# The output projection of a hybrid decoder block as seven half-size block products, with the sums of its operands on GpSimd and the row normalization one step earlier

## The chip, the core and the metric

The kernel runs on one core of a Trainium2 chip. The core has five engines that run their own instruction streams and wait for each other by semaphores: PE (TensorE, matmuls and transposes), DVE (VectorE), ACT (ScalarE), POOL (GpSimd) and SP (SyncE, which here only issues DMAs). The metric is the time of one execution on the device in microseconds, as the median of several runs. Names such as L167 are lines of the kernel before.

## What is computed

One decoder block on x of 1024 x 1024 in float32: two kinds of attention, their outputs gated and summed to y, an output projection with a residual, and a SwiGLU feed-forward with a residual. This is the part that matters:

```python
y = jax.nn.sigmoid(g_a) * (o_a @ w_o_swa[l]) + jax.nn.sigmoid(g_b) * (o_b @ w_o_mla[l])
x = x + y @ w_out[l]

h = rmsnorm(x, ffn_norm_g[l])
x = x + (jax.nn.silu(h @ w_gate[l]) * (h @ w_up[l])) @ w_down[l]
```

## The kernel before

**Products in three.** A float32 product is made of three matmuls in the format fp32r: an operand is split into a high part, a cast by ACT, and a low part, the operand less its high part, on DVE (`split`, L159), and `mm3` (L163) multiplies high by high, high by low and low by high into one PSUM bank. Every operand of every product costs one cast on ACT and one subtraction on DVE, which reads the operand and its high part, both in SBUF unless the operand is fresh in PSUM.

**Mix stage (L1302 to L1355).** Twelve steps, named in `steps` (L1317), make y transposed, 128 features by 1024 tokens at a time: step `a4` to `a7` the gated product with `w_o_swa`, step `b0` to `b7` (`mix_b`) the product with `w_o_mla`, its gate, the sum and the split of y. For features 0 to 3 the first gate's product is one POOL operation (L1308). Every half of 512 tokens costs 12 matmuls.

**Output projection (L1505 to L1549).** Four segments, each half of the rows by half of the columns, in row blocks of 128: eight blocks of y by w_out, three matmuls each, into a bank; DVE adds the bank to x (`add`, L1528). w_out comes in pieces by the class `Stream`, three rounds of four pieces of 128 x 1024, each split when it is next. In segments 1 and 3 a row is then complete: ACT makes its sum of squares (L1534), POOL two small operations (`rstd_of`, L299 and L302), DVE the normalized row `xn` (L1539). One row block later `to_h` (L1365) transposes it on PE, eight transposes, and makes the operands of the feed-forward.

**Feed-forward.** The class `Seven` multiplies by a scheme in which a 2 x 2 block product takes seven block products instead of eight, with sums of blocks as operands. A pair of column blocks has the index j, its seven products the numbers q, and each comes for the gate weights (g) and the up weights (u); `fa(0,5)` means the bank `fa`, pair 0, product 5. The weight sums are made by `mix` and their splits by `prep`; the sums of the activations (`t1` to `t4`) are made by `to_h`, its second part `rest` (held back by L1547), and `late_split` (L1497), from the raw copies `hraw`. In before the sums and low parts of the activations are on DVE, the weight sums of pair 0 on POOL, of pair 1 on DVE (`ffn.mix(1, nc.vector)`).

**What sets the order.** On SP the program's order. On the other engines a scheduler places the work by its own costs, but from segment 3 on, through the first products of the feed-forward, the order is the one written out by hand (`manual_schedule`, L1505). Each engine runs its instructions in its order, so an instruction that waits holds up all behind it.

Of the kernel before, what the change touches and what calls it, by code (L numbers as in the profile page):

```python
# [89 lines left out]
def hybrid_block_kernel(  # L90
# [1248 lines left out]
    new_quads("y")  # L1339
    for k, (what, dc) in enumerate(steps):  # L1340
# [11 lines left out]
        if k >= 8:  # L1352
            st.load_to(st.index[("out", 0, k - 8)])
        if k >= 9:
            st.conv_to(st.index[("out", 0, min(k - 9, 3))])  # L1355
    st.conv_to(st.index[("out", 0, 3)])


    fg_bc = bcast_gain("ffng", ffn_g)
# [5 lines left out]
    def to_h(xn, b):  # L1365
# [140 lines left out]
    prev = None  # L1506
    held = []
    for seg, (sh, hf) in enumerate(((0, 0), (0, 1), (1, 1), (1, 0))):
        if seg == 3:
# [4 lines left out]
        hs = half(hf)
        for b in range(4 * sh, 4 * sh + 4):
            if seg in (0, 2):
                x2[b] = load_x(b)
# [10 lines left out]
            add(x2[b][:, hs], ps, x2[b][:, hs], nc.vector)  # L1528
            if seg in (0, 2):
                st.conv_to(st.index[("out", seg // 2 + 1, b % 4)])  # L1530
            if seg in (1, 3):
                xn = U("xn")
                ss = tiny("ss")
                nc.scalar.activation(xn, x2[b], AF.Square, accum_out=ss)  # L1534
                rs = rstd_of(ss, D)
            lower = to_h(*prev) if prev is not None else None
            prev = None
            if seg in (1, 3):
                nc.vector.scalar_tensor_tensor(xn, x2[b], rs, fg_bc, op0=ALU.mult, op1=ALU.mult)  # L1539
                prev = (xn, b)  # L1540
                nc.sync.dma_start(x2_d[b], x2.pop(b))
# [10 lines left out]
    held.pop(0)()
    ffn.run()
    ffn.prep_to(4)
    held.pop(0)()
# [133 lines left out]
def _layouts(a):  # L1689
# [80 lines left out]
```

## Time and profile before

| | us |
|---|---|
| median of 3 runs (lowest, highest) | 1362.41 (1362.39, 1362.61) |
| span of the profiled execution | 1359.5 |
| PE busy in the span | 1339.6 (99%) |
| DVE, ACT, POOL busy | 912.7, 642.8, 557.7 |
| first matmul of the output projection, from the span's start | 627.06 |

The span is one profiled execution, from its first instruction to its last; the runs' times are those of whole executions. A timeline row has the start and the duration in us, the engine, the line, the operation, the tile written and those read, and, in brackets, how long the engine had been idle and what ended that. A group of rows has busy us, mean ns of one instruction, and the idle time before them. Names of tiles have no buffer numbers.

### The profile page before, as it was taken

To read this page: it belongs to the slowest core of one execution; us is meant where nothing else is said; L and a number is where in the kernel's file an instruction comes from. 1 tells how busy PE (TensorE), PEld (TensorE's weight loads), DVE (VectorE), ACT (ScalarE), POOL (GpSimd) and SP (SyncE) were. 2 spreads that over 40 slices of the span, in tenths; PEclk is the share of its full clock that TensorE was granted. 3 is DMA by queue.
4 is the path that set the end of the run, shared out by engine and by line. 5 is a ranking of instruction groups with operands and counts; after the bars stand their busy time and mean duration, and the time that the engine had idled before them with its cause. 6 is when DMAs were issued, how large, how long until landed. Compare 5 with 4: busy or idle time off the path is not lost.

```text
span 1359.5 us, 18989 instructions
## 1 busy us (share of the span) xinstructions
PE 1339.6 (99%) x6600; PEld 1120.0 (82%) x6600; DVE 912.7 (67%) x1495; ACT 642.8 (47%) x1299; POOL 557.7 (41%) x610
## 2 busy tenths in 40 slices
PE   9999999999999999999999999999999999999997
PEld 6899878878788888888887888888888888888886
DVE  7868767676777887585448866666656654664862
ACT  7434766675577776652336322323232332644453
POOL 2116645553166554200031465766665551022521
PEclk9999999999999999999999999999999999999999
DMA  9455322335100110671243353644434425996504
GB/s 366 154 189 163 119 86 82 113 117 182 51 2 13 44 47 17 241 239 63 105 174 132 119 181 139 235 178 169 152 144 171 170 83 183 375 382 246 170 9 147
DMA packets 78096, 202.25 MB, mean 149 GB/s; under 512 B 8753, under 2 KB 15409, under 8 KB 78001
## 3 DMA queue, kind: packets, MB, share of 16 engines
q1 hardware_dynamic: 77856, 201.04, 41.5%
q8 instruction: 52, 0.85, 0.3%
q14 instruction: 44, 0.35, 0.1%
q10 hardware_dynamic: 144, 0.00, 0.0%
HBM read 141.24 MB, written 59.77 MB: 148 GB/s over the span
## 4 chain that ended last, share of the span: by engine, by line
PE 88%; DVE 4%; issue 3%; POOL 2%; ACT 2%; DMA 0%; SPq 0%; POOLq 0%; ACTq 0%; DVEq 0%
PE fa L169 7%; PE fa L167 7%; PE fa L168 7%; PE fb L169 6%; PE fb L167 6%; PE fb L168 6%; PE fd L167 5%; PE fd L169 5%; PE fd L168 5%; PE pTb L1165 2%; PE xo L169 2%; PE xo L167 2%; PE xo L168 2%; PE ob L1188 1%; PE oA L167 1%
## 5 line engine op out<-in xcount | busy, mean ns | idle before, releaser
L161 DVE TENSOR_TENSOR wl<-wr,wl 128x512 fp32r<-128x512 f32 x150 | 153.6, 1048 | 72.2 <-ACT wl L160 71.9
L161 DVE TENSOR_TENSOR lrv<-lr,lrv 128x1024 fp32r<-128x1024 f32 x77 | 105.2, 1397 | 49.9 <-ACT lrv L160 48.8
L160 ACT CAST lrv<-lr 128x1024 fp32r<-128x1024 f32 x77 | 80.3, 1054 | 96.0 <-PE fd L169 56.0
L167 PE MATMUL fd<-lrv 128*128 128x512 f32 x308 | 119.8, 389 | 0.0
L168 PE MATMUL fd<-lrv 128*128 128x512 f32 x308 | 119.8, 389 | 0.0
L169 PE MATMUL fd<-lrv 128*128 128x512 f32 x308 | 119.8, 389 | 0.0
L172 POOL TENSOR_TENSOR wr<-wr,sm 128x512 f32<-128x512 f32 (+1 forms) x38 | 46.4, 1229 | 149.1 <-DVE wl L161 116.4
L160 ACT CAST wl<-wr 128x512 fp32r<-128x512 f32 x150 | 87.0, 624 | 2.4 <-DVE wr L820 2.2
L299 POOL TENSOR_SCALAR ms<-ss 128x1 f32<-128x1 f32 x32 | 8.8, 274 | 189.1 <-ACT xn L1534 111.7
L161 DVE TENSOR_TENSOR wl<-sm,wl 128x512 fp32r<-128x512 f32 x60 | 47.5, 818 | 45.1 <-ACT wl L160 45.0
L169 PEld LDWEIGHTS fd<-lrv 128*128 128x128 f32 x308 | 57.8, 188 | 12.1
L168 PEld LDWEIGHTS fd<-lrv 128*128 128x128 f32 x308 | 57.8, 188 | 12.1
L167 PEld LDWEIGHTS fd<-lrv 128*128 128x128 f32 x308 | 57.8, 188 | 11.8
L1150 POOL TENSOR_TENSOR denb<-denb,neg_one 128x1 f32<-128x1 f32 x64 | 36.5, 571 | 74.4 <-ACT p L1149 64.7
L1149 ACT ACTIVATE p<-scb,nmb 128x384 f32<-128x384 f32 (+3 forms) x64 | 47.6, 745 | 35.9 <-DVE nmb L1148 34.1
L161 DVE TENSOR_TENSOR ptl<-pTb,pth 128x512 fp32r<-128x512 f32 (+2 forms) x96 | 50.1, 550 | 13.8 <-ACT pth L160 13.0
L1148 DVE CUSTOM_DVE_ANT_0 scb<-scb,mask 128x384 f32<-128x384 f32 (+3 forms) x64 | 48.6, 759 | 14.0 <-PE scb L1140 13.7
L1426 ACT ACTIVATE act<-sm 128x512 f32<-128x512 f32 x11 | 7.0, 636 | 104.8 <-DVE sm L175 104.8
L1151 POOL TENSOR_SCALAR p<-p,denb 128x384 f32<-128x384 f32 (+3 forms) x64 | 49.8, 778 | 6.3
L160 ACT CAST pth<-pTb 128x512 fp32r<-128x512 f32 (+2 forms) x96 | 43.0, 483 | 13.6 <-PE pTb L1165 13.1
L167 PE MATMUL fb<-t2h,wl 128*128 128x512 f32 x120 | 47.4, 395 | 0.0
L167 PE MATMUL fb<-t3h,wl 128*128 128x512 f32 x120 | 47.3, 394 | 0.0
(346 smaller groups left out, 4287.3 us busy)
## 6 DMA issues: line engine op xcount, KB each, us to landing
lr<-la_d SPq DMA_DIRECT2D x77, 256.0 KB, 5.4
wr<-in_w_gate_dram SPq DMA_DIRECT2D x22, 512.0 KB, 3.8
wr<-in_w_up_dram SPq DMA_DIRECT2D x22, 512.0 KB, 5.0
wd<-in_w_down_dram SPq DMA_DIRECT2D x22, 512.0 KB, 6.8
rb_d<-wd SPq DMA_DIRECT2D x22, 512.0 KB, 2.6
la_d<-sd SPq DMA_DIRECT2D x22, 512.0 KB, 5.4
lr<-rb_d SPq DMA_DIRECT2D x44, 256.0 KB, 5.4
lr<-in_w_down_dram SPq DMA_DIRECT2D x33, 256.0 KB, 5.6
```

What stands on the lines that cost most here:

```text
L160: nc.scalar.copy(hi, src)
L161: (eng or nc.vector).tensor_tensor(lo, src, hi.bitcast(F32), op=ALU.subtract)
L167: nc.tensor.matmul(ps, ah, bh, start=first and i == 0, stop=False, skip_group_check=go_on)
L168: nc.tensor.matmul(ps, ah, bl, start=False, stop=False, skip_group_check=go_on)
L169: nc.tensor.matmul(ps, al, bh, start=False, stop=last and i == n - 1, skip_group_check=go_on)
L172: eng.tensor_tensor(out, a, b, op=ALU.subtract)
L1148: nc.vector.tensor_tensor_reduce(s_, s_, m_, 1.0, -NEG, op0=ALU.add, op1=ALU.min, accum_out=nm)
L1149: nc.scalar.activation(p_, s_, AF.Exp, scale=-1.0, bias=nm, accum_out=den)
L1150: nc.gpsimd.tensor_tensor(den, den, neg_one[:, 0:1], op=ALU.pow)
L1151: nc.gpsimd.tensor_scalar(p[:, 0:w], p[:, 0:w], den, 0.0, op0=ALU.mult, op1=ALU.add)
L1165: nc.tensor.transpose(pp[:, i], p[:, blk(k0 + i)], ident)
L1188: nc.tensor.matmul(po[:, q_off:], vst, lo[:, kb % 4, q_off:], start=False, stop=kb == nk - 1)
```

## The change

**Output projection.** It becomes the scheme of the feed-forward: y (two blocks of rows by two of the inner dimension) times w_out (two by two) by seven products in the order 1, 2, 6, 7, 5, 4, 3. A product has four row blocks of twelve matmuls. Products share banks: 1 and 2, then 5 and 3, in banks A; 6, 7 and 4 in banks B. Product 1 is also kept in SBUF (`p1o`, four ACT copies) and added to x by POOL during products 6 and 7, and every other bank is added to x by DVE when a product ends in it.

**Sums and splits.** `y_sums` makes four sums for each of four pairs of feature blocks, 16 POOL operations of 128 x 512; `w_sum` eight POOL operations of 128 x 1024. Each product has its own splits of its operands (four of y and two of w_out, product by product), of which products 1 and 2 have theirs in the mix stage, and the others by a list (`prep`) that is worked off at 1.9 items for each row block. w_out is loaded in four pieces of 1 MB during the mix stage. The mix steps come in another order, with features dc and dc+4 as neighbours, and the layout of `w_o_mla` fits that.

**Rows.** `row_sum`, `row_norm` and `next_h` take the place of the chain behind segments 1 and 3: a row's squares are made when it is complete, its normalized values one row block later, its transposes after that. The last three rows' transposes stand between the first products of the feed-forward.

**Engines.** To POOL go one subtraction of `hraw`, the low parts of `t3` and `t4`, and the weight sums of pair 1; `to_h` makes its splits ahead of its copies of `hraw`.

The core of the diff:

```diff
-        for sh in range(2):
+        for sh in (1, 0):
             cs = half(sh)
             pb = PX("oB")
...
-            split(*hT(dc, cs), ga[:, cs])
-    steps = ("a4", "b0", "b1", "a5", "b2", "b3", "a6", "b4", "a7", "b5", "b6", "b7")
+        y[dc] = ga
+        y_split((1, 2)[dc // 4], dc % 4)
+        if dc >= 4:
+            y_sums(dc - 4)
...
+    def y_sums(k):
...
+        add(s1, a21, a22, nc.gpsimd)
+        sub(s3, a11, a21, nc.gpsimd)
+        sub(a21, s1, a11, nc.gpsimd)
+        sub(a11, a12, a21, nc.gpsimd)
...
+    def w_sum(n, j):
...
+        sub(*{1: (t1s[j], b12, b11), 3: (b12, b22, b12), 2: (b11, b22, t1s[j]), 4: (b21, b21, b11)}[n], nc.gpsimd)
...
+    steps = ("a4", "b0", "b4", "a5", "b1", "b5", "a6", "b2", "b6", "a7", "b3", "b7")
+    W_LOAD = {4: (0, 0), 5: (0, 1), 6: (1, 1), 8: (1, 0)}
+    W_WORK = {7: [(w_split, 1)], 9: [(w_sum, 1)], 10: [(w_sum, 3)], 11: [(w_split, 2), (w_sum, 2)]}
...
-        sub(r[:, 1], r[:, 1], t23[:, 0], nc.vector)
+        sub(r[:, 1], r[:, 1], t23[:, 0], nc.gpsimd)
...
-            split_h(name, c, r[:, i])
+            split_h(name, c, r[:, i], (nc.vector, nc.gpsimd)[i])
...
+    X_ORDER = (1, 2, 6, 7, 5, 4, 3)
...
+    def xo_done(q, t):
+        ps = bank["A" if q in (1, 2, 5, 3) else "B"][t]
+        if q == 1:
+            nc.scalar.copy(p1o[:, t], ps)
+        else:
+            residual(*{2: (4 + t, 0), 6: (4 + t, 1), 7: (t, 1), 5: (t, 1), 4: (t, 0), 3: (4 + t, 1)}[q], ps, nc.vector)
+        if q in (6, 7):
+            residual({6: 4, 7: 0}[q] + t, 1, p1o[:, t], nc.gpsimd)
+        if q == 7:
+            residual(t, 0, p1o[:, t], nc.gpsimd)
...
+    for q in X_ORDER:
...
+        for t in range(4):
...
+            if (q, t) == (5, 3):
                 ffn.mix(0)
...
+            mm3(bank["A" if q in (1, 2, 5, 3) else "B"][t],
+                [((ah[:, k, blk(t)], al[:, k, blk(t)]), (bh[:, k], bl[:, k])) for k in range(4)],
+                first=q in (1, 6, 5), go_on=q in (2, 7, 4, 3))
+            xo_done(q, t)
+            if q == 1 and t < 2:
+                w_sum(4, t)
+            n_x += q != 1
+            while prep and 30 - len(prep) < 1.9 * n_x:
+                f, q_, j = prep.pop(0)
+                f(q_, j)
+            r = {4: 0, 3: 4}.get(q)
+            if r is not None:
+                if q == 3:
+                    next_h()
+                row_sum(r + t)
+                if r + t >= 1:
+                    row_norm(r + t - 1)
+                if (q, t) == (4, 2):
+                    next_h()
...
     ffn.prep_to(14)
-    ffn.mix(1, nc.vector)
+    ffn.mix(1)
```

POOL in the mix stage and ahead of it, before: the last softmax normalizations of the attention (`p`), the four gate products (`sg<-ar,sg`), and behind them the small operations of the projection's rows.

```order
310 L1151 TENSOR_SCALAR p_6357<-p_6357,denb_6358 128x768
311 L1308 TENSOR_TENSOR sg_6510<-ar_6155,sg_6510 128x1024
312 L1308 TENSOR_TENSOR sg_6528<-ar_6195,sg_6528 128x1024
313 L1308 TENSOR_TENSOR sg_6601<-ar_6364,sg_6601 128x1024
314 L1308 TENSOR_TENSOR sg_6643<-ar_6448,sg_6643 128x1024
315 L299 TENSOR_SCALAR ms_7166<-ss_7164 128x1
316 L302 TENSOR_TENSOR rstd_7168<-ms_7166,neg_half 128x1
```

After, from the same gate product on. `ys` are the sums of y, `wt` and `wo` those of w_out; the pair of `sg` names in a row are features dc and dc+4.

```order
311 L1304 TENSOR_TENSOR sg_6510<-ar_6155,sg_6510 128x1024
312 L1304 TENSOR_TENSOR sg_6590<-ar_6195,sg_6590 128x1024
313 L175 TENSOR_TENSOR ys_6631<-sg_6510,sg_6508 128x512
314 L172 TENSOR_TENSOR ys_6632<-sg_6510 128x512
315 L172 TENSOR_TENSOR sg_6510<-ys_6631,sg_6510 128x512
316 L172 TENSOR_TENSOR sg_6510<-sg_6508,sg_6510 128x512
317 L1304 TENSOR_TENSOR sg_6713<-ar_6364,sg_6713 128x1024
318 L172 TENSOR_TENSOR ys_6632<-sg_6590 128x512
319 L175 TENSOR_TENSOR ys_6631<-sg_6590,sg_6552 128x512
320 L172 TENSOR_TENSOR sg_6590<-ys_6631,sg_6590 128x512
321 L172 TENSOR_TENSOR sg_6590<-sg_6552,sg_6590 128x512
322 L1304 TENSOR_TENSOR sg_6842<-ar_6448,sg_6842 128x1024
```

Between and behind the gate products stand the sums; sixteen of y, and six of w_out before the last of these.

DVE at the start of the feed-forward, before: `pu` and `sm<-fb` are evictions of the bank `fb` (products 6 and 7), `t1l` and `t4l` low parts of the activations' sums, `wl` low parts of weights, `sm<-wr` weight sums. `wl_7938` and `wl_7941` are the operands of `fa(0,5)`.

```order
1030 L175 TENSOR_TENSOR pu_7747<-fb_7920,pu_7747 128x512
1031 L161 TENSOR_TENSOR t1l_7870<-hraw_7379,t1h_7869 128x4x128
1032 L161 TENSOR_TENSOR t4l_7874<-hraw_7379,t4h_7873 128x4x128
1033 L161 TENSOR_TENSOR wl_7938<-sm_7458,wl_7938 128x512
1034 L161 TENSOR_TENSOR wl_7941<-sm_7462,wl_7941 128x512
1035 L175 TENSOR_TENSOR sm_7944<-wr_7707,wr_7710 128x512
1036 L175 TENSOR_TENSOR sm_7458<-fb_7902,pu_7726 128x512
1037 L172 TENSOR_TENSOR sm_7944<-sm_7944,wr_7707 128x512
1038 L172 TENSOR_TENSOR wr_7707<-wr_7707 128x4x128
```

After, the same products; the operands of `fa(0,5)` are `wl_7984` and `wl_7987`.

```order
1036 L175 TENSOR_TENSOR pu_7729<-fb_7932,pu_7729 128x512
1037 L161 TENSOR_TENSOR t1l_7903<-hraw_7594,t1h_7902 128x4x128
1038 L161 TENSOR_TENSOR wl_7951<-wr_7325,wl_7951 128x512
1039 L175 TENSOR_TENSOR sm_7387<-fb_7910,pu_7709 128x512
1040 L161 TENSOR_TENSOR t1l_7903<-hraw_7636,t1h_7902 128x4x128
1041 L161 TENSOR_TENSOR wl_7999<-wr_7347,wl_7999 128x512
1042 L161 TENSOR_TENSOR wl_8002<-wr_7348,wl_8002 128x512
1043 L175 TENSOR_TENSOR sm_7391<-fb_7932,pu_7729 128x512
1044 L161 TENSOR_TENSOR wl_7984<-sm_7387,wl_7984 128x512
1045 L161 TENSOR_TENSOR wl_7987<-sm_7391,wl_7987 128x512
```

The `t4l` and the `sm<-wr` sums have left DVE, the `wl` of `fa(0,5)` stand behind both evictions of product 7, and the `wl` of `fa(0,5)` and `fb(0,4)` have changed places.

PE at the same place, before: `fa(0,5)` for gate runs whole.

```order
3558 L169 MATMUL fb_7920<-t3h_7580,wl_7882 128x512
3559 L167 MATMUL fa_7985<-t1h_7869,wl_7938 128x512
3560 L168 MATMUL fa_7985<-t1l_7870,wl_7938 128x512
3561 L169 MATMUL fa_7985<-t1h_7869,wl_7938 128x512
3562 L167 MATMUL fa_7985<-t1h_7869,wl_7938 128x512
3563 L168 MATMUL fa_7985<-t1l_7870,wl_7938 128x512
```

After, right behind the last matmul of `fb(0,7)` for up: two matmuls each of `fa(0,5)` for gate and up, three of `fb(0,4)`, and then the first L169 of `fa(0,5)`, the one that multiplies by the low part of `wl_7984`.

```order
3511 L167 MATMUL fa_8005<-t1h_7902,wl_7984 128x512
3512 L168 MATMUL fa_8005<-t1l_7903,wl_7984 128x512
3513 L167 MATMUL fa_8024<-t1h_7902,wl_7987 128x512
3514 L168 MATMUL fa_8024<-t1l_7903,wl_7987 128x512
3515 L167 MATMUL fb_7910<-t4h_7906,wl_7999 128x512
3516 L168 MATMUL fb_7910<-t4l_7907,wl_7999 128x512
3517 L169 MATMUL fb_7910<-t4h_7906,wl_7999 128x512
3518 L169 MATMUL fa_8005<-t1h_7902,wl_7984 128x512
3519 L167 MATMUL fa_8005<-t1h_7902,wl_7984 128x512
```

Seven matmuls now stand between the end of `fb(0,7)` and the first that reads the low part of `wl_7984`, and this order is the scheduler's, behind the written one's end.

POOL at the start of the feed-forward, after: low parts of `t3` and `t4`, the weight subtractions of pair 0 (`wr<-wr,sm`), and the sums of pair 1.

```order
372 L172 TENSOR_TENSOR t3l_7680<-t_1454_7805,t3h_7679 128x4x128
373 L172 TENSOR_TENSOR hraw_7636<-hraw_7636,t_1462_7860 128x512
374 L172 TENSOR_TENSOR t3l_7680<-t_1462_7860,t3h_7679 128x4x128
375 L161 TENSOR_TENSOR t4l_7907<-hraw_7494,t4h_7906 128x4x128
376 L161 TENSOR_TENSOR t4l_7907<-hraw_7549,t4h_7906 128x4x128
377 L172 TENSOR_TENSOR wr_7347<-wr_7347,sm_7387 128x4x128
378 L161 TENSOR_TENSOR t4l_7907<-hraw_7594,t4h_7906 128x4x128
379 L172 TENSOR_TENSOR wr_7348<-wr_7348,sm_7391 128x4x128
380 L161 TENSOR_TENSOR t4l_7907<-hraw_7636,t4h_7906 128x4x128
381 L175 TENSOR_TENSOR sm_7990<-wr_7523,wr_7568 128x512
382 L172 TENSOR_TENSOR sm_7990<-sm_7990,wr_7523 128x512
```

In before there stand between the last row's small operations and the first `wd` operation only four rows there, all of weights:

```order
335 L299 TENSOR_SCALAR ms_7685<-ss_7683 128x1
336 L302 TENSOR_TENSOR rstd_7687<-ms_7685,neg_half 128x1
337 L172 TENSOR_TENSOR wr_7421<-wr_7421,sm_7458 128x4x128
338 L172 TENSOR_TENSOR wr_7422<-wr_7422,sm_7462 128x4x128
339 L172 TENSOR_TENSOR wr_7710<-wr_7710,sm_7944 128x4x128
340 L172 TENSOR_TENSOR wr_7710<-wr_7710,sm_7948 128x4x128
341 L172 TENSOR_TENSOR wd_8019<-wd_8019 128x512
```

The rows of `t3l` and `t4l` and the sums `sm` have moved to POOL, ahead of the `wd` operations.

## Rows read from the trace of the kernel before

**Rows 1.** The page: its first line, and PE and POOL of its parts 1 and 2.

```profile
span 1359.5 us, 18989 instructions
...
PE 1339.6 (99%) x6600; PEld 1120.0 (82%) x6600; DVE 912.7 (67%) x1495; ACT 642.8 (47%) x1299; POOL 557.7 (41%) x610
...
PE   9999999999999999999999999999999999999997
...
POOL 2116645553166554200031465766665551022521
```

**Rows 2.** Stretches: busy us (count) of PE, PEld, DVE, ACT, POOL; clock, DMA share, GB/s.

```profile
567.00:627.07 60.07, 60.07 (x267) 49.76 (x266) 46.25 (x59) 32.41 (x39) 9.59 (x4) 1.00 0.66 233
627.07:727.00 99.93, 99.09 (x466) 82.36 (x465) 50.66 (x63) 30.32 (x54) 16.56 (x23) 1.00 0.33 127
727.00:800.00 73.00, 72.58 (x321) 59.00 (x320) 60.20 (x82) 30.39 (x55) 31.18 (x21) 1.00 0.36 124
```

**Rows 3.** What PE waited for, 690 to 900 us: us, times, longest.

```profile
PE tp L1372 <- DVE xn L1539: 0.8, 1, 0.8
PE fa L167 <- ACT wl L160: 0.3, 1, 0.3
PE fa L169 <- DVE wl L161: 0.2, 1, 0.2
```

**Rows 4.** Timeline of PE: start, us, line, operation, tiles.

```profile
627.06 0.39 PE L167 MATMUL xo<-wv,yh 128*128 128x512 f32 x1
...
656.98 0.39 PE L167 MATMUL xo<-wv,yh 128*128 128x512 f32 x1
...
659.70 1.03 PE L1372 MATMUL tp<-ident,xn 128*128 128x128 f32 x8
660.50 0.48 PE L167 MATMUL xo<-wv,yh 128*128 128x512 f32 x1
```

**Rows 5.** Groups by line and shape, 567.00 to 627.07: busy, mean ns, idle before.

```profile
L1308 POOL TENSOR_TENSOR sg<-ar,sg 128x1024 f32<-128x1024 f32 x4 | 9.6, 2408 | 24.1 <-ACT sg L1221 24.1
...
L161 DVE TENSOR_TENSOR wl<-wr,wh 128x1024 fp32r<-128x1024 f32 x4 | 4.9, 1220 | 0.6 <-ACT wh L160 0.6
```

**Rows 6.** Timelines of DVE and POOL, 786 to 797.

```profile
786.68 0.69 DVE L175 TENSOR_TENSOR sm<-fa,sm 128x512 f32<-128x512 f32 x1 [2.03 <-PE fa L169]
786.92 1.30 POOL L172 TENSOR_TENSOR sm<-sm,wr 128x512 f32<-128x512 f32 x1
...
791.25 3.31 POOL L172 TENSOR_TENSOR wd<-wd,wd 128x512 f32<-128x512 f32 x2
791.65 5.16 DVE L161 TENSOR_TENSOR wl<-wr,wl 128x512 fp32r<-128x512 f32 x3
```

**Rows 7.** Timelines of DVE and POOL, 574 to 582.

```profile
574.98 2.41 POOL L1308 TENSOR_TENSOR sg<-ar,sg 128x1024 f32<-128x1024 f32 x1 [3.19 <-ACT sg L1221]
575.73 2.20 DVE L161 TENSOR_TENSOR yl<-sg,yh 128x512 fp32r<-128x512 f32 x1 [0.69 <-ACT yh L160]
...
580.38 0.69 DVE L161 TENSOR_TENSOR yl<-sg,yh 128x512 fp32r<-128x512 f32 x1
```

**Rows 8.** DMA issues from 560 to 800: KB each, median us to landing.

```profile
wr<-in_w_out_dram SPq DMA_DIRECT2D x12, 512.0 KB, 6.7
```

**Rows 9.** Timelines of PE and DVE at a row of the projection's end.

```profile
701.41 0.39 PE L167 MATMUL xo<-wv,yh 128*128 128x512 f32 x1
701.61 0.69 DVE L175 TENSOR_TENSOR x<-xo,x 128x512 f32<-128x512 f32 x1 [3.62 <-PE xo L169]
...
704.57 1.28 DVE L1539 SCALAR_TENSOR_TENSOR xn<-x,rstd,ffng 128x1024 f32<-128x1024 f32 x1 [2.27 <-POOL rstd L302]
```

**Rows 10.** Timelines of DVE, POOL and PE, 753 to 757.

```profile
753.13 1.29 DVE L161 TENSOR_TENSOR wl<-sm,wl 128x512 fp32r<-128x512 f32 x2
...
756.45 2.13 POOL L172 TENSOR_TENSOR wr<-wr,sm 128x512 f32<-128x512 f32 x1 [25.93 <-DVE sm L172]
756.56 0.39 PE L167 MATMUL fa<-t1h,wl 128*128 128x512 f32 x1
```

More of the change, by code (lines that the diff above doesn't have):

```diff
@@ L1302, in mix_b @@
     def mix_b(dc):
-        if dc % 2 == 0:
-            wo["b"] = st.get(("ob", dc // 2))
+        if dc < 4:
+            wo["b"] = st.get(("ob", dc))
         w = wo["b"]
@@ new lines, in y_sums, with w_load @@
+    def y_sums(k):
+        if k == 0:
+            y_new.extend([V("ys") for _ in range(2)])
+        s1, s3 = y_new[0][:, k], y_new[1][:, k]
+        a21, a11, a22, a12 = y[k][:, half(0)], y[k][:, half(1)], y[4 + k][:, half(0)], y[4 + k][:, half(1)]
+        add(s1, a21, a22, nc.gpsimd)
+        sub(s3, a11, a21, nc.gpsimd)
+        sub(a21, s1, a11, nc.gpsimd)
+        sub(a11, a12, a21, nc.gpsimd)
+    wr, wl, t1s = {}, {}, {}
+    def w_load(i, d):
+        wr[(i, d)] = V("wo")
+        nc.sync.dma_start(wr[(i, d)], w_out[i, d])
@@ new lines, in w_split @@
+    def w_split(q, j):
+        k = slice(2 * j, 2 * j + 2)
+        if j == 0:
+            wl[q] = (V("woh", F32R), V("wol", F32R))
+        key = {1: (0, 0), 2: (1, 0), 6: (0, 0), 7: (0, 1), 5: None, 4: (1, 0), 3: (1, 1)}[q]
+        hi, lo = wl[q]
+        split(hi[:, k], lo[:, k], t1s[j] if q == 5 else wr[key][:, k])
+    def w_sum(n, j):
+        k = slice(2 * j, 2 * j + 2)
+        if n == 1:
+            t1s[j] = U("wt", F32, (P, 2, 512))
+        b11, b12, b21, b22 = (wr.get((i, d)) for i in range(2) for d in range(2))
+        b11, b12, b21, b22 = (None if w is None else w[:, k] for w in (b11, b12, b21, b22))
+        sub(*{1: (t1s[j], b12, b11), 3: (b12, b22, b12), 2: (b11, b22, t1s[j]), 4: (b21, b21, b11)}[n], nc.gpsimd)
@@ L1328, in weights_of @@
         if k < len(steps):
-            return st.index[("o" + steps[k][0], int(steps[k][1]) // 2)]
+            what, dc = steps[k][0], int(steps[k][1])
+            return st.index[("o" + what, dc // 2 if what == "a" else dc % 4)]
         return -1
@@ L1351, in hybrid_block_kernel @@
         st.conv_to(weights_of(k + 1))
[L1352 to L1359, printed above, removed]
+        if k in W_LOAD:
+            w_load(*W_LOAD[k])
+        for f, q in W_WORK.get(k, ()):
+            for j in range(2):
+                f(q, j)
     raw1 = {}
@@ new lines, in hybrid_block_kernel, with residual @@
+    p1o = V("xp1")
+    X_ORDER = (1, 2, 6, 7, 5, 4, 3)
+    xns = []
+    rests = []
+    def residual(b, d, src, eng):
+        add(x2[b][:, half(d)], src, x2[b][:, half(d)], eng)
+    def xo_done(q, t):
[8 more added lines that the diff above has]
+            residual(t, 0, p1o[:, t], nc.gpsimd)
@@ L1528, in hybrid_block_kernel @@
[L1528 to L1541, printed above, removed]
@@ L1550, in hybrid_block_kernel @@
+            if (q, t) in PREP:
+                ffn.prep_to(PREP[q, t])
     ffn.n_ahead = 1
     ffn.run()
[L1552 to L1555, printed above, removed]
+    row_norm(7)
+    ffn.prep_to(5)
     ffn.run()
     ffn.prep_to(6)
-    lower = to_h(*prev)
+    next_h()
+    rests.pop(0)()
     ffn.run()
+    rests.pop(0)()
+    ffn.prep_to(7)
     ffn.run()
-    lower()
     ffn.prep_to(8)
-    for i in range(1, 6):
+    next_h()
+    ffn.run()
+    rests.pop(0)()
+    ffn.prep_to(9)
@@ L1564, in hybrid_block_kernel @@
+    ffn.run()
+    next_h()
+    ffn.run()
+    rests.pop(0)()
+    ffn.prep_to(10)
+    ffn.run()
+    for i in range(1, 5):
+        late_split(i - 1)
         if i == 2:
-            ffn.prep_to(10)
+            ffn.prep_to(11)
         if i == 3:
```

96 lines of the change are left out of this document (57 added, 39 removed).

## The prediction

> **What bounds the kernel now.** I read the page first: the profiled execution spans 1359.5 us and PE is busy in 1339.6 of them, nine tenths or more in every slice but the last, while POOL is busy in one to three tenths of many [rows 1]. Its outputs are timed at 1362.41 us, so 2.9 us lie outside the span, and I make the sum on the span and add them. Then the table of stretches: in the mix stage (567.00 to 627.07) PE is busy in 60.07 of 60.07 us, in the projection with its transposes in 99.09 of 99.93, in the start of the feed-forward in 72.58 of 73.00 [rows 2]. The list of PE's waits from 690 to 900 has three entries, 1.3 us in all [rows 3]. So in the part that changes PE hides everything else, and the time is the number of PE instructions by their spacing. A recorded matmul lasts 0.39 us, but twelve of them begin from 656.98 to 659.70: 2.72 / 12 = 0.2267 us each. Eight transposes take 659.70 to 660.50, 0.80 us [rows 4]. The other engines matter only where PE has nothing left to run before an operand arrives.
>
> **What the change takes off PE.** Before: 4 segments x 4 row blocks x 8 k x 3 = 384 matmuls 128x512. After: 7 products x 4 row blocks x 4 k x 3 = 336. Transposes, mix matmuls and feed-forward matmuls keep their number. 48 x 0.2267 = **10.9 us** off PE, all of it on the path, as PE is the path. Of the three old waits, the 0.8 us for a normalized row [rows 3] loses its cause (a row now has a product of slack), so -0.8 at best. Best possible: -11.7.
>
> **What it adds elsewhere, and where that meets PE.** I call the first projection matmul E (627.06 before [rows 4]) and lay the products end to end: 10.88 us each, with 0.80 to 0.88 for eight transposes.
>
> *Mix stage, up to E.* POOL did four products of 2.41 us there, 9.6 us [rows 5]. Now it does these four, 16 sums of y (128x512, 1.30 each by the nearest POOL rows [rows 6]) and, before product 1, six of the eight sums of w_out (128x1024, 2.41): 9.6 + 20.8 + 14.5 = 44.9 us of 60. That alone fits, and product 6, the first to use them, begins at E + 21.8. What they do to DVE is the question. Beside POOL's sum at 574.98, DVE's `yl<-sg,yh`, two operands in SBUF, takes 2.20 us; at 580.38, with POOL idle, the same instruction takes 0.69 [rows 7]. Later, with POOL busy without a gap, three such subtractions take 5.16 us, 1.72 each, and POOL's own rows lengthen from 1.30 to 1.66, while the add at 786.68, with one operand from PSUM, takes 0.69 beside POOL's row at 786.92 [rows 6]. So two-SBUF work of DVE and POOL's work take turns. The Trainium skill, page "SBUF — State Buffer", section "Who interferes with whom", says the same as a rule: a DVE instruction with two SBUF inputs and a GpSimd instruction that reads SBUF contend for a shared port pair that one holds for a whole instruction, and the other fully blocks. These rows agree (2.20 against 0.69). It speaks against giving POOL sums beside a busy DVE; what it would make of the time at its full length is the slower rival below.
>
> DVE's own work in the stage: 24 evictions from PSUM and 24 two-SBUF operations of 0.69 each (16 adds, 8 `yl`), and 8 wide splits of 1.22 [rows 5]: 33.1 + 9.8 = 42.9 us of 60. If each of the 32 two-SBUF operations lost 1.72 - 0.69 = 1.03 us in POOL's share of the time (44.9 / 60 = 0.75), DVE would need 42.9 + 24.7 = 67.6 us, 7.5 over. The bounds at this seam are 0 and 7.5. Going through the two engines in program order, each blocked operation waiting for the rest of the other's, I find the last `yl` of product 1 near E + 1 where PE asks for it at E + 2.3 (the twelve matmuls of a row block go k by k), and that of product 2 some 0.2 us late. I take **1 us**, near the lower end, because POOL sits idle between steps waiting for y and DVE catches up then. The fourth load of w_out, 1 MB, is issued near the stage's end, after step `b6`; 0.5 MB of w_out landed in 6.7 us [rows 8], and ACT's cast of it stands ahead of the cast of `yh` for `b3`. At 10 to 13 us it just arrives; if not, it adds up to 3 us, inside the same bounds.
>
> *Products 6, 7, 5.* The 14 splits of w_out and 28 of y (before: 12 and 16) and 24 evictions instead of 16 go to ACT and DVE; both have the room (DVE was busy in 50.66 of 99.93 us [rows 2]), and the operands of a product are split during the one before. POOL adds `p1o` 4 times in product 6 and 8 times in product 7: 8 x 1.3 = 10.4 of 10.9 us. Costed at nothing; PE's cover is a product long.
>
> *Rows and transposes.* In before the way from a finished block to its normalized row is: matmuls of the next group at 701.41, `x` at 701.61, `rstd` in time for `xn` at 704.57, which lasts 1.28 us [rows 9]: 4.4 us. The new order gives each row the next block's matmuls as cover, 2.7 us or more. Only row 0 is tight: POOL's six instructions of `mix(0)` stand ahead of its `rstd`, and its transposes come one block after it. 0 to 0.8 us; I take **0.4**.
>
> *Start of the feed-forward, E + 100 to E + 127.* DVE loses 18 operations of 0.69 (`t4l`, `t3l`, one subtraction of `hraw`, four each, and `mix(1)`, six): 12 us less. POOL gains them at 1.30: 23 us, and its two `wr` subtractions, into a stretch in which it was idle for 25.93 us [rows 10]. In before the two `wl<-sm` splits for `fa(0,5)` end at 754.4 [rows 10], with PE reaching that product at 756.56, 2 us later. After, DVE's order has, behind the eviction of `fb(0,7)` for gate: `t1l`, two `wl` of `wr`, the eviction of `fb(0,7)` for up, and only then `wl_7984`. Say T is when PE begins the group after `fb(0,7)` for up. Its order then allows 7 matmuls, 1.59 us, before the one that needs the low half of `wl_7984`. An eviction begins 0.20 us behind the next group's start [rows 9]. With DVE alone the three operations (back to back 0.60 apiece: two take 1.29 [rows 10], of which the second 0.69) end at T - 2.72 + 0.20 + 0.60 + 1.8 = T - 0.1, the eviction at T + 0.8, the split at T + 1.5: in time by 0.1. With POOL busy throughout they take 1.72 each: T + 3.2, eviction T + 3.8, split T + 5.5, **3.9 us late**. The same lock on the earlier `t1l` and `wl` puts the operands of `fb(0,7)` 0 to 2 us late. Bounds 0 and 6; since POOL has 25 us of work in 27 us I take **4**, nearest to [rows 6].
>
> The sum: -10.9 - 0.8 + 1 + 0.4 + 4 = -6.3, span 1353.2, time 1353.2 + 2.9 = **1356.1 us** (-0.46%). Later stages keep their work and order.
>
> **Rivals.** (a) The lock is milder than my walk, or slack absorbs it, and nearly all of the 10.9 comes through: -9 to -11.7, 1350.7 to 1353.4, about 1351.5. For it: from 690 to 900 PE waits 0.5 us for `wl` in all [rows 3], though the slow splits of [rows 6] lie in that stretch. Against: there a `wl` is split a product or more ahead of PE, here 7 matmuls ahead. (b) **Slower**: the lock decides both seams at its upper price. DVE comes 7.5 us late to E, the feed-forward pays 6, row 0 pays 0.8: -10.9 + 14.3 = +3.4, 1365.8. It decides from the point at which stalls pass 10.9 us; it needs POOL to hold SBUF in the whole of both stretches, against the idle time between steps in the first. This is also the case in which the rule of the Trainium skill's page "SBUF — State Buffer" ("the other **fully blocks**") would hold at every instruction of both stretches. (c) The middle: the load of w_out late by 3 us or the mix seam at half its bound, with 4 to 6 at the feed-forward: -10.9 + 4 + 0.4 + 5 = -1.5, 1360.9, no change that can be told. (d) The change doesn't shorten PE: excluded, since the new loop has 7 x 4 groups of 12 matmuls and nothing else is given to PE.
>
> **Chances and range.** A measurement of this kernel can tell about 0.2%, 2.7 us, from no change. Forecast (-3 to -9): 0.57. Rival (a): 0.20. Middle (c) and its neighbours within 2.7 us: 0.12. Slower (b): 0.11. So faster 0.77, same 0.12, slower 0.11. The range takes in the forecast, (a) and most of (c): 1350.7 to 1361.2; (b) and the last of (c) are left out, some 0.15.
>
> **What would show it.** In the new trace: xo matmuls 336 and spaced 0.2267; the product block shorter by 10.9 from its first to its last matmul if no seam stalls; `yl` at the end of the mix at over 1.5 us each beside POOL; PE waits named `fa` or `fb` for DVE's `wl` of 1 to 4 us some 100 to 120 us after E; `tp` waiting for `xn` at most 0.8. Wrong if PE's waits from 620 to 760 sum to under 2 us (rival a) or over 8 (c, b), or if waits appear inside products 6 to 5, for POOL's adds, where I saw none.

## The result, and the profile after

The changed kernel takes 1367.41 us (median of 5, 1366.06 to 1367.46) against 1362.39: a ratio of 1.0033, 95% interval 1.0022 to 1.0044. It is **slower by 5.0 us**, where 1356.1 and at most 1361.2 were forecast. The page of its profiled execution, the lines that answer to [rows 1] (from here on, line numbers in rows are those of the kernel that ran):

```profile
span 1365.7 us, 18965 instructions
...
PE 1331.8 (98%) x6552; PEld 1112.6 (81%) x6552; DVE 954.9 (70%) x1499; ACT 652.0 (48%) x1317; POOL 657.6 (48%) x664
```

PE does what was forecast, 48 instructions less, and is busy 7.8 us less, not 10.9; the span is 6.2 longer. DVE is now at 70% and POOL at 48%. The first projection matmul begins at 628.9 in this execution (627.06 before, [rows 4]) and the first matmul of the down projection, of which nothing was changed, at 1149.0:

```profile
L167 PE MATMUL xo<-woh,yh x112: 389/389/774, 628.9 to 717.7; 128*128 128x512 f32 x112
L167 PE MATMUL fd<-lrv x308: 389/389/389, 1149.0 to 1357.8; 128*128 128x512 f32 x154
```

Before, that last row began at 1142.8. So the changed stretch, from the one to the other, took 515.7 us and takes 520.1: 4.4 more. The 1.8 us by which its start has moved lie ahead of the mix stage, in which PE has no gap, in PE waits (`kvq` 0.9 us before and 2.2 now, `k` 1.5 and 2.2). In the eleven traces of the experiments below, whose edits all lie behind that start, it falls anywhere from 626.5 to 629.6; that is why I compare this stretch, and the timed medians, rather than spans.

What PE waits for, first from 600 to 730 and then from 730 to 1000 (us, times, longest), to be read beside [rows 3]:

```profile
PE tp L1422 <- DVE xn L1588: 5.6, 1, 5.6
PE xo L169 <- DVE yl L161: 1.0, 1, 1.0
...
PE fa L169 <- DVE wl L161: 2.6, 1, 2.6
PE fb L169 <- DVE wl L161: 1.7, 2, 1.3
PE fa L167 <- ACT pu L793: 1.6, 1, 1.6
PE fb L168 <- DVE t2l L172: 0.3, 1, 0.3
PE fb L167 <- DVE pu L175: 0.2, 1, 0.2
```

These add to 13.0 us, where before had 1.3. With the 10.9 us saved that makes +0.8; most of the rest of the 4.4 is the clock. PE around the longest wait:

```profile
692.59 0.39 PE L169 MATMUL xo<-woh,yl 128*128 128x512 f32 x1
698.59 1.97 PE L1422 MATMUL tp<-ident,xn 128*128 128x128 f32 x8 [5.61 <-DVE xn L1588]
700.21 0.77 PE L167 MATMUL xo<-woh,yh 128*128 128x512 f32 x1
...
704.04 0.40 PE L167 MATMUL xo<-woh,yh 128*128 128x512 f32 x1
```

After 5.61 us of idleness the eight transposes take 1.62 us (698.59 to 700.21) where they took 0.80 [rows 4], and the nine matmuls behind them take 3.83 us (700.21 to 704.04) instead of 9 x 0.2267 = 2.04. That is 2.6 us more. The granted clock (behind the five engines' busy times) in stretches of 4 us says the same, 0.63 and 0.52 of the full 2.4 GHz, so the lower level of 1.2 GHz for most of that time; from 704 to 708 it is 1.00 again:

```profile
648.00:694.00 46.00, 44.98 (x199) 36.91 (x197) 45.71 (x44) 15.81 (x23) 33.20 (x19) 1.00 0.07 23
696.00:700.00 4.00, 1.41 (x7) 1.41 (x8) 3.37 (x5) 1.68 (x4) 1.17 (x3) 0.63 0.42 171
700.00:704.00 4.00, 4.00 (x12) 3.21 (x11) 2.89 (x4) 3.23 (x6) 0.74 (x2) 0.52 0.68 221
704.00:708.00 4.00, 4.00 (x22) 3.31 (x20) 2.23 (x3) 1.21 (x3) 0.74 (x2) 1.00 0.88 306
```

The first row of that table shows where to look: from 648 to 694, from within product 2 to the pause of PE in product 4, DVE is busy in 45.71 of 46.00 us. What it does at the end of that stretch:

```profile
689.67 2.31 DVE L161 TENSOR_TENSOR wol<-wo,woh 128x1024 fp32r<-128x1024 f32 x1
...
693.60 0.68 DVE L175 TENSOR_TENSOR x<-xo,x 128x512 f32<-128x512 f32 x1
...
697.26 1.27 DVE L1588 SCALAR_TENSOR_TENSOR xn<-x,rstd,ffng 128x1024 f32<-128x1024 f32 x1
```

The eviction at 693.60 is the last of row 0. PE had ended that block at 687.4. DVE is 6.2 us late, and everything behind it (squares, `rstd`, `xn` at 697.26, the transposes at 698.59) is late with it. Of that stretch, the groups by line and shape (busy, mean ns | idle before):

```profile
L175 POOL TENSOR_TENSOR x<-xp,x 128x512 f32<-128x512 f32 x12 | 22.2, 1872 | 12.6 <-ACT yh L160 10.1 <-ACT woh L160 1.3 <-DVE x L175 1.2
L161 DVE TENSOR_TENSOR yl<-sg,yh 128x512 fp32r<-128x512 f32 x11 | 13.6, 1251 | 0.0
...
L161 DVE TENSOR_TENSOR wol<-wo,woh 128x1024 fp32r<-128x1024 f32 x7 | 11.7, 1668 | 0.0
```

A `yl` takes 1251 ns instead of 690 [rows 7], a wide `wol` 1668 instead of 1220 [rows 5], and POOL's additions of `p1o` 1872 instead of 1300 [rows 6].

### The profile page after: what moved, and what is told of

Its sections match the earlier page's. It is cut to its first block, busy times and chain, and to the rows that moved or that the text cites. A ratio compares the mean times of both kernels' runs of the same rounds, so it can differ in the third digit from the quotient of the medians.

```text
span 1365.7 us, 18965 instructions
## 1 busy us (share of the span) xinstructions
PE 1331.8 (98%) x6552; PEld 1112.6 (81%) x6552; DVE 954.9 (70%) x1499; ACT 652.0 (48%) x1317; POOL 657.6 (48%) x664
## 5 line engine op out<-in xcount | busy, mean ns | idle before, releaser
L161 DVE TENSOR_TENSOR wl<-wr,wl 128x512 fp32r<-128x512 f32 x150 | 156.4, 1064 | 76.6 <-ACT wl L160 76.3
L169 PE MATMUL fd<-lrv 128*128 128x512 f32 x308 | 119.8, 389 | 0.0
L161 DVE TENSOR_TENSOR wl<-sm,wl 128x512 fp32r<-128x512 f32 x60 | 53.4, 915 | 45.5 <-ACT wl L160 45.5
L169 PEld LDWEIGHTS fd<-lrv 128*128 128x128 f32 x308 | 57.8, 188 | 11.9
L175 POOL TENSOR_TENSOR du<-du,xq 128x512 f32<-128x512 f32 x8 | 16.3, 2054 | 69.5 <-DMA lr<-in_w_down_dram 50.4
L1478 ACT ACTIVATE act<-pu 128x512 f32<-128x512 f32 x22 | 13.9, 632 | 74.7 <-DVE pu L175 74.7
```

The source lines that it names most:

```text
L161: (eng or nc.vector).tensor_tensor(lo, src, hi.bitcast(F32), op=ALU.subtract)
L169: nc.tensor.matmul(ps, al, bh, start=False, stop=last and i == n - 1, skip_group_check=go_on)
L175: eng.tensor_tensor(out, a, b, op=ALU.add)
L1478: nc.scalar.activation(dst, src, AF.Silu)
```

## The experiments

All runs are compared with the kernel before, run beside them. All times are medians; intervals are 95%.

**Without the additions of product 1.** The 12 POOL operations go, nothing replaces them, so that a part of x is missing.

```diff
-        if q in (6, 7):
-            residual({6: 4, 7: 0}[q] + t, 1, p1o[:, t], nc.gpsimd)
-        if q == 7:
-            residual(t, 0, p1o[:, t], nc.gpsimd)
```

> The changed kernel without the 12 POOL additions of p1o to x (they are left out, so a part of the residual's sum is missing). The changed kernel takes 1367.4 us; in its trace PE waits 5.6 us for row 0's xn and runs its next matmuls at half clock, some 2.8 us more, while DVE has no gap from 648 to 694 and stores the sum of row 0 some 6.5 us after PE has made it. Theory A (POOL's two-operand work blocks DVE's two-operand work): DVE gets back about 12 x 1.1 us, the wait falls to 0 to 1 us, the half clock goes with it: about 1359.5. Theory B (POOL's own queue: its adds and mix(0) stand ahead of row 0's rstd): the same 1359 to 1360, but DVE's two-operand rows stay as slow as they are. Theory C (DVE has too much work of its own, 24 evictions, 20 yl, 10 wol): the wait stays at 4 us or more, 1366 to 1367.

Measured: 1358.83 us, ratio 0.9972 (0.9962 to 0.9983). The `tp` wait and the half clock behind it are gone, the other waits are the same to 0.2 us. Its DVE from 648 to 694:

```profile
648.00:694.00 46.00, 46.00 (x208) 38.18 (x207) 39.38 (x48) 18.28 (x29) 11.46 (x10) 1.00 0.14 48
```

DVE has 6.6 us to spare in the stretch, with all its own work. Theory C, that its own work is too much, is out as a cause by itself. A and B are not told apart yet.

**The same additions on DVE, and the sums of `mix(0)` on DVE.**

```diff
-            residual({6: 4, 7: 0}[q] + t, 1, p1o[:, t], nc.gpsimd)
+            residual({6: 4, 7: 0}[q] + t, 1, p1o[:, t], nc.vector)
...
-            residual(t, 0, p1o[:, t], nc.gpsimd)
+            residual(t, 0, p1o[:, t], nc.vector)
```

> The 12 additions of p1o on DVE instead of POOL, nothing else. Theory A: DVE does 12 x 0.6 = 7.2 us more and is blocked some 13 us less, so row 0 is 0 to 3 us late instead of 5.6: 1360 to 1363. Theory B: POOL is free and the wait is gone: 1359.5. Theory C: DVE, already full, gets 7.2 us more, the wait grows to 10 us or more: 1373 to 1376.

```diff
-                ffn.mix(0)
+                ffn.mix(0, nc.vector)
```

> The six sums of mix(0) on DVE instead of POOL, nothing else. Theory A: DVE does 6 x 0.6 = 3.6 us more and is blocked about 6.6 us less, the adds of p1o still block it: row 0 still 2 to 4 us late, 1363 to 1366. Theory B: nothing stands ahead of row 0's rstd on POOL, the wait goes: 1359 to 1360. Theory C: the wait grows to 9 us: 1370 to 1372.

Measured: 1367.31 (1.0034, 1.0020 to 1.0049) and 1367.93 (1.0037, 1.0022 to 1.0052): both as the changed kernel. The `tp` wait is 5.1 and 5.8 us. Theory B falls with this: in the first POOL does no addition of `p1o`, in the second no `mix(0)`, and row 0 waits all the same. Theory A as I had put it falls too, since it promised a gain for both, and theory C promised a loss of several us for both. In the first run, the groups of DVE over the same 46 us, and PE's wait:

```profile
L175 DVE TENSOR_TENSOR x<-xp,x 128x512 f32<-128x512 f32 x12 | 11.3, 970 | 0.3
...
L161 DVE TENSOR_TENSOR wol<-wo,woh 128x1024 fp32r<-128x1024 f32 x7 | 9.6, 1370 | 0.0
L161 DVE TENSOR_TENSOR yl<-sg,yh 128x512 fp32r<-128x512 f32 x11 | 8.9, 824 | 0.0
PE tp L1422 <- DVE xn L1588: 5.1, 1, 5.1
```

The additions cost DVE 11.3 us. Its `yl<-sg` fell from 13.6 to 8.9, `yl<-ys` from 9.7 to 5.3 (its row is left out here), `wol` from 11.7 to 9.6 and the other two `wol` from 3.5 to 2.4: 12.3 us back. What 12 operations on POOL take from DVE by blocking and what they cost on DVE itself come out nearly equal, about 1 us for each. So I formed theory D: for work with two operands in SBUF the two engines are nearly **one server**, and moving work from one to the other changes nothing while it is full. Read again, what is full is DVE itself, more than the turns of the two: by the times that rows have alone, DVE's own work with the additions is 43.3 us of the 46 (35.0, as summed up further down, and 12 x 0.69), and only seven rows of 1.30 are left to POOL.

**Another order, same work.** The list of splits is worked off at a pace; at 1.9 it is empty before product 4 begins, and all splits of product 3 stand ahead of row 0's eviction.

```diff
-            while prep and 30 - len(prep) < 1.9 * n_x:
+            while prep and 30 - len(prep) < 1.6 * n_x:
```

> The changed kernel with one number changed: the list of splits for products 6 to 3 is worked off at 1.6 items for each row block instead of 1.9, so that most splits of the last product (3) no longer stand ahead of the eviction of row 0's last block on DVE. All work stays, POOL's too. Theory D (new: DVE and POOL are together about full from product 2 on, and the order decides; splits that nobody needs yet stand ahead of row 0): row 0 comes 4 to 7 us earlier, the wait of 5.6 us falls to 0 to 1.5 and the half clock goes: 1359 to 1361. Theory A (blocking alone, whatever the order): no gain, 1366 to 1368.

Measured: 1364.88 (1.0021, 1.0012 to 1.0031), by the ratios 1.6 us less than the changed kernel, with intervals that overlap; the `tp` wait is 4.2. Theory D's 1359 to 1361 is missed, and so is theory A's figure. The order has a part in the wait, less than I expected. Row 0's eviction begins at 688.33, 2.7 us after PE had ended that block instead of 6.2, but `xn` gains only 1.4 of the 3.5 us: ACT's squares end at 690.24, and now POOL's `mix(0)` is ahead of `rstd`, with its last row ending at 691.26 and `ms` at 691.35 behind it, and `xn` then begins at 694.07, behind a split on DVE. So theory B's queue is there, and shows once DVE is less late. The kernel stays slower than before.

**POOL busy, but reading nothing.** The 12 additions become 12 memsets.

```diff
-            residual({6: 4, 7: 0}[q] + t, 1, p1o[:, t], nc.gpsimd)
+            nc.gpsimd.memset(p1o[:, 0:2], 0.0)
...
-            residual(t, 0, p1o[:, t], nc.gpsimd)
+            nc.gpsimd.memset(p1o[:, 2:4], 0.0)
```

> The 12 POOL additions of p1o are replaced by 12 POOL memsets of 128 x 1024 into p1o (the additions are left out, so a part of the residual's sum is missing). POOL is busy there, but reads nothing from SBUF. If DVE is blocked because POOL reads SBUF: DVE's yl take 0.69 beside the memsets, the time is that of the kernel without the additions, 1358.8 (within 0.7). If any busy POOL slows DVE: yl take 1.2 us or more beside the memsets, and the time lies between 1361 and 1367.

Measured: 1362.98 (1.0005, 0.9995 to 1.0014). The time lies in the range of the second expectation, but not for its reason: POOL ran the memsets in one piece, and ACT's next cast waited 12.3 us for the last of them, which held up DVE by 7.6 us. The durations do answer the question, POOL's row first:

```profile
649.31 5.00 POOL L1574 MEMSET xp<- 128x1024 f32 x5
651.04 1.21 DVE L161 TENSOR_TENSOR wol<-wo,woh 128x1024 fp32r<-128x1024 f32 x1
652.17 0.68 DVE L161 TENSOR_TENSOR yl<-sg,yh 128x512 fp32r<-128x512 f32 x1
```

Beside five memsets in a row a `wol` takes 1.21 and a `yl` 0.68 us, their times alone; later in the same trace, beside `mix(0)`, a `wol` takes 2.31 (680.53) and a `yl` 1.78 (677.13) again. So in these rows it is POOL's reading that blocks, not its being busy. The Trainium skill, page "SBUF — State Buffer", section "Who interferes with whom", says that a DVE instruction with two SBUF inputs contends with a GpSimd instruction that reads SBUF and not with one that only writes; these rows agree.

**The sum complete, without POOL and without DVE.** ACT, which is busy in 15.8 of these 46 us, already copies product 1 out of PSUM. It now copies it into the banks of product 6, and products 6, 7 and 4 accumulate onto it.

```diff
-            nc.scalar.copy(p1o[:, t], ps)
+            nc.scalar.copy(bank["B"][t], ps)
...
-                first=q in (1, 6, 5), go_on=q in (2, 7, 4, 3))
+                first=q in (1, 5), go_on=q in (2, 6, 7, 4, 3))
```

with the 12 additions left out and the banks taken ahead of product 1.

> The changed kernel with the complete sum, but without its 12 POOL additions: ACT copies product 1 into the PSUM banks of product 6 instead of SBUF, and products 6, 7 and 4 accumulate onto it. Theory D (DVE and POOL together are full from product 2 to 4, so only work that leaves both of them helps): as the kernel with the additions left out, 1358.8 within 1 us, the tp wait of 5.6 us and the half clock gone. If that kernel was fast only for another reason (an order of the scheduler that came with it): 1363 or more.

Measured: **1359.29 us**, ratio 0.9974 (0.9964 to 0.9984), faster than both. Its waits, from 600 to 735 and from 735 to 1000, and DVE's stretch:

```profile
PE fa L167 <- ACT pu L793: 1.6, 1, 1.6
...
PE fa L169 <- DVE wl L161: 2.6, 1, 2.6
PE fb L169 <- DVE wl L161: 1.7, 2, 1.3
648.00:694.00 46.00, 46.00 (x208) 38.18 (x207) 39.39 (x49) 18.29 (x29) 11.45 (x10) 1.00 0.13 46
```

The same sum in the same products, with 22.2 us of POOL work taken away and not put on DVE, takes 8.1 us less (8.0 by the ratios). That is what theory D forecast, and the kernel without the additions was not fast for what it left out. Nor was it another order: from 15 us behind the first projection matmul to row 0's `xn`, DVE's rows stand in the same order in the changed kernel and in both of these, and `xn` begins 68.3 us behind that matmul in the first and 62.3 and 62.4 in the other two. By itself it doesn't tell theory D from A, which would have gained here too; the two runs with work moved to DVE do.

**The start of the feed-forward.** Its waits add to 6.4 us in the changed kernel. DVE ahead of the wait of 2.6 us, and the matmul that waited:

```profile
756.82 0.68 DVE L175 TENSOR_TENSOR sm<-fb,pu 128x512 f32<-128x512 f32 x1
757.42 1.18 DVE L161 TENSOR_TENSOR t1l<-hraw,t1h 128x512 fp32r<-128x512 f32 x1
758.52 3.47 DVE L161 TENSOR_TENSOR wl<-wr,wl 128x512 fp32r<-128x512 f32 x2
761.91 0.68 DVE L175 TENSOR_TENSOR sm<-fb,pu 128x512 f32<-128x512 f32 x1
762.51 2.84 DVE L161 TENSOR_TENSOR wl<-sm,wl 128x512 fp32r<-128x512 f32 x2
763.71 0.50 PE L169 MATMUL fa<-t1h,wl 128*128 128x512 f32 x1 [2.61 <-DVE wl L161]
```

This is the step on T of the prediction (T is when PE begins the group after `fb(0,7)`): an eviction of `fb(0,7)` at 756.82, a `t1l` and two `wl` at 1.2 to 1.7 us each, the second eviction at 761.91, and `wl<-sm` behind it. First, all engines as in the kernel before:

```diff
-        sub(r[:, 1], r[:, 1], t23[:, 0], nc.gpsimd)
+        sub(r[:, 1], r[:, 1], t23[:, 0], nc.vector)
...
-                                   ("t3", t23[:, 1], nc.gpsimd)):
+                                   ("t3", t23[:, 1], nc.vector)):
...
-            split_h(name, c, r[:, i], (nc.vector, nc.gpsimd)[i])
+            split_h(name, c, r[:, i], nc.vector)
...
-    ffn.mix(1)
+    ffn.mix(1, nc.vector)
```

> The start of the feed-forward as in the kernel before as to engines: the subtraction of hraw, t3l, t4l and mix(1) on DVE, the rest as changed. In the changed kernel PE waits 6.4 us there (fa and fb for wl 4.3, for pu 1.6, small ones 0.5). Theory A: DVE does 18 x 0.6 = 11 us more, but its 20 or so two-operand operations are no longer slowed from 0.6 to 1.7: the waits fall to 1 to 2 us, 1362 to 1364. Theory C (the work of DVE itself): the waits grow to 8 us or more, 1369 or more.

Measured: 1366.99 (1.0031, 1.0021 to 1.0041), no gain, and between the two expectations. PE's waits, and the stretch from 738 to 748:

```profile
PE fa L167 <- ACT pu L793: 3.3, 1, 3.3
PE fb L169 <- DVE wl L161: 1.1, 1, 1.1
PE fa L169 <- DVE wl L161: 0.5, 1, 0.5
738.00:748.00 10.00, 8.05 (x23) 6.42 (x24) 9.08 (x15) 7.54 (x14) 0.00 (x0) 0.66 0.03 13
```

The waits for `wl` fall from 4.3 to 1.6, as theory A had it, but the wait for ACT's copy `pu` grows from 1.6 to 3.3, and the granted clock falls to 0.66 behind it. That wait lies at 740, ahead of all of `t4l`, and by the rows comes from the new order itself: `fa(1,2)` stands right behind the last transposes, and ACT's copy of its bank stands behind `t<-tp`, which waits for DVE's `hraw`. Why it grew by 1.7 was not tried by itself; in this trace three operations that POOL had done (one `hraw`, two `t3l`, 0.68 to 0.69 each) stand on DVE ahead of that `hraw`. Then the splits of `fa(0,5)` one product earlier, with the pace of 1.6:

```diff
         if i == 3:
             ffn.prep_to(12)
+        if i == 4:
+            ffn.prep_to(14)
         ffn.run()
-    ffn.prep_to(14)
```

> The pace of 1.6, and the splits for fa(0,5) made one product earlier, ahead of the eviction of fb(0,7) for up. The wait of 2.6 us of fa for wl should go or fall under 1 us if it comes from the place of wl_7984 in DVE's order, as my step on T has it; the other waits at the start of the feed-forward (fb for wl 1.7, fa for pu 1.6) stay: 2 to 2.6 us less than the kernel with the pace alone, 1356.5 to 1359. If POOL's load alone sets it, the stall only moves to the next product and the time stays within 0.7 us of the kernel with the pace alone.

Measured: 1365.12 (1.0019, 1.0010 to 1.0028), the same as with the pace alone.

```profile
PE fb L167 <- DVE pu L175: 2.4, 1, 2.4
PE fb L169 <- DVE wl L161: 1.7, 2, 1.3
PE fa L169 <- DVE wl L161: 0.4, 1, 0.4
```

`fa` for `wl` falls from 2.6 to 0.4, and a wait of 2.4 for the eviction, which is now the later one, takes its place. As with the additions, order alone only moves it while DVE is full.

Three more kernels have product 1 in PSUM and change the sums of pair 1: later (the line is left out, and the planner asks for them two products on), on DVE, and on DVE with `t4l`.

```diff
-    ffn.mix(1)
```

> Product 1 in PSUM, and the six POOL sums of pair 1 (mix(1)) made some two products later, where the planner asks for them, instead of ahead of fa(0,5). If POOL's load just there delays the splits of fa(0,5): its wait of 2.6 us falls under 1 us, and 1.5 to 2.5 us less than with product 1 in PSUM alone, unless pair 1's fb product then waits for the sums (then no gain, 0 to 3 us more).

```diff
-    ffn.mix(1)
+    ffn.mix(1, nc.vector)
```

> Product 1 in PSUM, and mix(1) on DVE as in the kernel before; t3l, t4l and hraw stay on POOL. Theory D: a POOL operation takes DVE's turn for about 1.1 us and does what DVE does in 0.6, so DVE is no later with six operations more: the waits of fb and fa for wl (4.3 us) fall to 2 to 3 us, 1 to 2 us less than with product 1 in PSUM alone. If DVE's own load counts: 2 to 4 us more.

```diff
-            split_h(name, c, r[:, i], (nc.vector, nc.gpsimd)[i])
+            split_h(name, c, r[:, i], nc.vector)
...
-    ffn.mix(1)
+    ffn.mix(1, nc.vector)
```

> Product 1 in PSUM, mix(1) and t4l on DVE; t3l and one subtraction of hraw stay on POOL. Theory D: POOL is nearly idle while the splits of fa(0,5) are made, no two-operand row of DVE there takes over 1.3 us, the waits of fb and fa for wl fall to 0 to 2 us: 2 to 4 us less than with product 1 in PSUM alone. If DVE's own load counts: 3 us or more above it.

Measured: 1358.03 (0.9966, 0.9953 to 0.9979), 1358.23 (0.9963, 0.9950 to 0.9976) and 1358.09 (0.9967, 0.9955 to 0.9978). All are about 1 us below the 1359.29 of product 1 in PSUM alone, and their intervals overlap with its own, so neither a gain over it nor an order among the four is shown. In the first, the waits from 735 on:

```profile
PE fb L169 <- DVE wl L161: 1.7, 2, 1.3
PE fa L169 <- DVE wl L161: 1.5, 1, 1.5
PE fb L167 <- DVE pu L175: 0.7, 1, 0.7
```

`fa` for `wl` is 1.5 instead of 2.6, and 0.7 has come up at the next product. In the other two it is 0.5, while `fb` waits 2.8 and 2.2 for `wl` instead of 1.7. If shortening a stall of this kind gives anything back here, it is some 1 us, and not the 1.5 to 4 that the first and the third expectation had; it turns up in part at the next product.

## Why the prediction was wrong

*PE's saving: right.* 336 matmuls, spaced 0.2267 where nothing waits; -10.9.

*The mix stage: right in size, in part by luck.* I took 1 us between bounds of 0 and 7.5; PE waits 1.0 for `yl`, once. But the walk had product 1's last `yl` in time, at E + 1, and product 2's 0.2 late, and it is product 1's that came late, at E + 3.7:

```profile
628.00 1.05 ACT L160 CAST woh<-wo 128x1024 fp32r<-128x1024 f32 x1 [7.53 <-DMA wo<-in_w_out_dram]
629.61 2.95 DVE L161 TENSOR_TENSOR yl<-sg,yh 128x512 fp32r<-128x512 f32 x1 [1.62 <-ACT yh L160]
```

ACT's cast of the last piece of w_out waited for its load until 628.00, the cast of `yh` stood behind it, and the `yl` then took 2.95 us beside POOL's `w_sum`. So the load that the prediction called just in time has a part in this 1 us; how large a part was not tried.

*Products 6, 7, 5: the step that failed.* I costed them at nothing, because DVE had been busy in 50.66 of 99.93 us in [rows 2] and every product had a product's time of cover. I had the slow two-operand rows of [rows 6] in hand and used them in the mix stage and at the feed-forward's start, but not here, where POOL was given 12 additions (22.2 us as they ran) beside the `mix(0)` that it had there before (now 11.3 us, two of each kind at 3.5, 4.3 and 3.5), and DVE 19 splits of y, where before had two (627 to 693). The old average of an engine says nothing about a stretch to which the change gives other work. The right sum was at hand: evictions 16 x 0.68, `yl` 19 x 0.69 and `wol` 9 x 1.22 make DVE's own 35.0 us of the 46, and POOL's 19 rows at 1.30 [rows 6] make 24.7, which have to take turns with the 24.1 of these that have two operands in SBUF: 48.8 if every eviction runs beside a POOL row, and 59.7 if none does, both over 46. Measured, DVE's 44 instructions of the stretch add to 49.4 us of durations (10.9 + 13.6 + 9.7 + 11.7 + 3.5; neighbours overlap by some 0.08 us) where 35.0 are their own, and DVE ends 6.2 us late. With the additions taken off both engines the kernel takes 1359.29, 3.5 us less than before and inside the range that was stated, so this step with what follows from it is what put the time outside.

*Row 0: mis-sized by that.* 0.4 was taken, 0 to 0.8 the bounds; 5.6 measured. POOL's `mix(0)` ahead of `rstd`, which I had named as the tight place, is not what it waited for: in the changed kernel `ms` begins at 695.60, released by ACT's squares, 0.8 after the last `mix(0)` row has ended. The bound came from the order on POOL, and the eviction of the row on DVE was taken to be on time. The tight place is real behind it: with the pace of 1.6, where that eviction is earlier, `ms` did wait for `mix(0)`.

*The clock: missing.* I had no term for what a long stall costs after it ends. It cost 2.6 us here, nearly half of the wait itself.

*The start of the feed-forward: the mechanism right, the size low.* I took 4 us between 0 and 6; 6.4 came, over the upper bound: 2.6 at `fa(0,5)` (3.9 worked out at full blocking), 1.7 at `fb(0,7)` (0 to 2 worked out), and 1.6 for ACT's `pu`, with 0.5 small ones, which I had not seen: a wait on ACT behind a transpose, from the order and not from POOL.

*The sum as measured:* -10.9 - 1.3 + 1.0 + 5.6 + 6.4 + 2.6 = +3.4, against +4.4 in the stretch; 1.0 is left. Some 0.8 of it lies in how a wait is counted: from the end of the matmul ahead, which lasts 0.39 us, though the next could have begun 0.2267 behind its start, so each wait costs 0.16 us more than it is listed with (from 692.59 to 698.59 it is 6.00 - 0.23 = 5.77, and 5.61 is listed), and there are eight waits where before had three. Rival (b) named the right mechanism, and the wrong place: it had the price at E and at the feed-forward, and not between them; that its +3.4 equals this sum is chance. Its chance of 0.11 was too low because the price of blocking had been put on two of the three stretches in which POOL gets work.

## What to carry to other kernels

When work is moved to POOL to relieve DVE, add DVE's whole work and POOL's instructions that read SBUF, each at the time that it has alone, stretch by stretch with the new work in it, and compare the sum with PE's time for the stretch. As an estimate from the rows here, that is 59.7 of 46 us for the changed kernel (35.0 + 19 x 1.30), 52.4 with the 12 additions on DVE (43.3 + 7 x 1.30) and 44.1 without them (35.0 + 7 x 1.30): only the last kept up. Moving the additions either way changed nothing (1367.3 and 1367.4), and taking them off both gave 8 us. The turns of two-operand work alone would have misled: 48.8 (24.1 + 24.7) and 41.5 (24.1 + 8.3 + 9.1), and the second was late as well. Look for work that an idle engine or an accumulation already does for free: ACT writing product 1 into the bank that the next products add onto turned a loss of 5.0 us into a gain of 3.5. A PE stall of several us should also be given a term for the slower clock behind it.

## What the runs showed of the hardware

The granted clock behind a stall: after 5.6 us of waiting it was 0.63 and 0.52 in two stretches of 4 us, and 1.00 in the next. In the kernel with the feed-forward's work on DVE it was 0.66 from 738 to 748, around a wait of 3.3 us. A wait of 2.6 us for the same operand was followed by 1.00 in the changed kernel (first row) and by 0.66 with product 1 in PSUM (second row):

```profile
764.00:768.00 4.00, 4.00 (x19) 3.27 (x19) 2.04 (x2) 0.90 (x2) 4.00 (x4) 1.00 0.01 4
755.00:760.00 5.00, 5.00 (x17) 3.90 (x16) 1.91 (x2) 0.78 (x2) 5.00 (x5) 0.66 0.01 3
```

So one and the same wait was followed by the lower clock in one kernel and not in the other; these runs don't show why.

PE accumulates onto a bank that ACT has written: products 6, 7 and 4 began with no start flag on the copy of product 1, with no wait of PE for it and an unchanged spacing. All four banks had been written by matmuls of the mix stage before; a bank that no matmul had written was not tried, so nothing is shown for it.
